# Sliding-window attention in pairs of steps: the same matmuls, grouped in sixteen rounds instead of thirty-two steps

## The chip, the cores and the metric

One core of a Trainium2 chip runs the kernel. A core has five engines with queues of their own: TensorE (PE) multiplies matrices, VectorE (DVE), ScalarE (ACT) and GpSimd (POOL) work elementwise, and SyncE (SP) issues most of the transfers. The metric is the time of one execution on the device, in microseconds (us); the median of three runs is given.

## What is computed

A trunk of two layers over 1024 tokens of width 1024, all in float32. Layer one is a gated linear recurrence, layer two is attention in a window of 128 keys; a gated feed-forward part with a short convolution follows each. The change lies in the attention of layer two, sixteen query heads of 64 that share four key and value heads:

```
def swa_sink_mixer(h, k, v, w_q, sinks, bias, mask, w_out):
    q = (h @ w_q).reshape(B, nb, SW_WINDOW, SW_KV_HEADS, SW_GROUP, SW_HEAD_DIM)
    ...
    kk, vv = with_prev(k), with_prev(v)
    logits = jnp.einsum('bntgrd,bnsgd->bngrts', q, kk).astype(jnp.float32) * scale
    ...
    logits = jnp.where(mask[None, :, None, None], logits, -jnp.inf)
    m = jnp.maximum(logits.max(-1), sink)
    p = jnp.exp(logits - m[..., None])
    denom = p.sum(-1) + jnp.exp(sink - m)
    o = jnp.einsum('bngrts,bnsgd->bntgrd', p, vv.astype(jnp.float32))
    o = o / jnp.moveaxis(denom, -1, 2)[..., None]
    return o.reshape(B, S, D).astype(h.dtype) @ w_out
```

Each query sees itself and the 127 tokens before it. `with_prev` puts the keys of the block before ahead of a block's own. So of the 256 keys that a block of 128 queries is multiplied with, exactly 128 count per query, the upper triangle of one block and the lower triangle of the other.

## The kernel before

**Precision.** A float32 product is made from three fast matmuls (`mm3`, lines 188 to 192): both operands are split into a high part and a low rest, and high by high, high by low and low by high are added. So every operand of a projection is first cast (ACT) and its low rest subtracted (DVE, `low_part`, line 162, which the profile shows as L164). The casts of weights from their raw tiles are line 171, other casts line 216. `T` holds the layer's input so, `HL` the weights.

**The attention, before.** The heads are taken in eight pairs, `c` = 0 to 7, and each pair in four steps `bp` of two blocks of 128 queries. `attend` (line 1299) is a generator that records one step in seven stages, with a `yield` after each:

1. Queries by keys on PE (line 1310, eight matmuls into one `psax` tile), and a copy of the diagonal block's logits to `X` on ACT (line 1313).
2. DVE copies the earlier block's logits into `X` under a triangular mask (line 1317), so that `X` holds each query's 128 valid logits; in a pair's first step, which has no earlier block, POOL masks (line 1320) instead. POOL adds the bias (line 1323).
3. DVE takes the maximum `nm` (lines 1328, 1331); `se`, the sink's part, is made on POOL for `c` up to 5, else on DVE (line 1332); ACT takes four exponentials of 128 by 128, each with its sum (line 1335), and the sink's (line 1337).
4. DVE makes the sum, its reciprocal and the product (lines 1339 to 1341).
5. PE transposes `X` in four (line 199).
6. DVE takes the two triangles apart into `W` (line 1349, two of 128 by 512); `W` is `W0` or row 7 of `Y`.
7. PE multiplies by the values (line 195, shown as sixteen records), and ACT copies the result to `Y` (line 1362), or, for the last pair, splits it into `T`.

**The fill.** Beside a step PE works on the next pair's queries: `q_proj` (line 1275) is a generator too, a half of the tokens takes eight `mm3` of 512 columns, and a quarter of a pair's 48 matmuls stands beside each step. `q_split` (line 1291) scales the finished half on ACT (line 1294, two) and takes its low part on DVE (line 1296, two). For the last pair the fill is the beginning of the output projection (`last_filler`, line 1376, which calls `out_part`). `q_unit` (line 1267) loads and splits a pair's query weights two pairs ahead; `out_unit` does so for the output weights.

**The order.** The order of PE, ACT, DVE and POOL in this part is the program's own, written out by hand: the loop over `c` and `bp` (line 1427) has up to three steps in flight beside the new one. In a step it records stages 1 and 2 of the new step, 7 of the step three back, 3 of the last one (ahead of the new one's stage 2), 5 and 6 of the step two back, a quarter of the fill, 4 of the last one, then splits of queries and a low part of a weight. `moves` (line 1425) says before which steps a part of `Y` is split into `T` for the output projection. What is left of the last three steps is written out behind the loop (line 1460 on), between parts of the output projection. Then `ffn` begins with `out_proj` (line 334), which adds the last head pair's part, and reads the residual rows that SP loads to `Y`.

**Buffers.** `X` has four buffers, `q` three, `psax` two of two PSUM banks and `psmm` four of one bank. A `psmm` bank serves in turn a half of the query projection, the transposes and the values.

Of the kernel before, what the change touches and what calls it, by code (L numbers as in the profile page):

```python
# [10 lines left out]
F32 = mybir.dt.float32  # L11
F32R = mybir.dt.float32r
U8 = mybir.dt.uint8
AF = mybir.ActivationFunctionType
# [93 lines left out]
def trunk(ctx: ExitStack, tc: tile.TileContext, a: dict, out: bass.AP):  # L108
# [1096 lines left out]
    with (tc.tile_pool(name="ta", bufs=1, reuse_waits="tile") as raws,  # L1205
# [90 lines left out]
                nc.vector.scalar_tensor_tensor(q[os, e, :], ps[es], 0.125, q[es, e, :].bitcast(F32),  # L1296
                                               op0=ALU.mult, op1=ALU.subtract)

        def attend(c, bp, q):
            pp, r = divmod(c, 4)  # L1300
            ps = psax()
            pv = ps.rearrange("p (e j s) -> p e j s", e=2, j=2)
            for low in range(2):
                for jj in range(2):
                    j = 2 * bp + jj
                    lo = P if j == 0 else 0
                    qs, ks = slice((j % 4) * P, (j % 4 + 1) * P), slice((j - 1) * P + lo, (j + 1) * P)
                    for e in range(2):
                        es = slice(64 * e, 64 * e + 64) if low else slice(0, P)
                        nc.tensor.matmul(pv[:, e, jj, lo:], q[bp // 2][es, e, qs],  # L1310
                                         Kl[es, pp, ks] if low else Kh[:, pp, e, ks], start=not low and jj == 0, stop=bool(low) and jj == 1)
            X = at.tile([P, 2, 2, P], F32, name="X", bufs=4)
            nc.scalar.copy(X, pv[:, :, :, P:])
            yield
            j0 = 1 if bp == 0 else 0
            for e in range(2):
                nc.vector.copy_predicated(X[:, e, j0:, :], msk[:, 7 * BL:].unsqueeze(1).to_broadcast([P, 2 - j0, P]),
                                          pv[:, e, j0:, :P])
                if j0:
                    nc.gpsimd.affine_select(out=X[:, e, 0, :], in_=X[:, e, 0, :], compare_op=ALU.is_ge,  # L1320
                                            fill=NEG, base=0, pattern=[[-1, P]], channel_multiplier=1)
            bv = bfs[c]
            nc.gpsimd.tensor_tensor(X, X, bv.unsqueeze(2).to_broadcast([P, 2, 2, P]), op=ALU.add)
            yield
            nm = sm.tile([P, 2, 2], F32, name="nm")
            se = sm.tile([P, 2, 2], F32, name="se")
            dn = sm.tile([P, 2, 2], F32, name="dn")
            nc.vector.tensor_reduce(nm, X, axis=mybir.AxisListType.X, op=ALU.max)
            skv = sk[:, 8 * pp + r:8 * pp + r + 5:4].unsqueeze(2).to_broadcast([P, 2, 2])
            nsv = nsk[:, 8 * pp + r:8 * pp + r + 5:4].unsqueeze(2).to_broadcast([P, 2, 2])  # L1330
            nc.vector.scalar_tensor_tensor(nm, nm, -1.0, nsv, op0=ALU.mult, op1=ALU.min)
            (nc.vector if c > 5 else nc.gpsimd).tensor_tensor(se, skv, nm, op=ALU.add)
            for e in range(2):
                for jj in range(2):
                    nc.scalar.activation(X[:, e, jj, :], X[:, e, jj, :], AF.Exp, bias=nm[:, e, jj:jj + 1],
                                         accum_out=dn[:, e, jj:jj + 1])
            nc.scalar.activation(se, se, AF.Exp)
            yield
            nc.vector.tensor_tensor(dn, dn, se, op=ALU.add)
            nc.vector.reciprocal(dn, dn)  # L1340
            nc.vector.tensor_tensor(X, X, dn.unsqueeze(3).to_broadcast([P, 2, 2, P]), op=ALU.mult)
            yield
            pt = psmm()
            for i in range(4):
                tr(pt[:, i * P:(i + 1) * P], X[:, i // 2, i % 2, :])
            yield
            W = W0 if bp % 2 else Y[:, NB - 1, :].rearrange("p (k g s) -> p k g s", k=2, g=4)
            for k in range(2):
                nc.vector.tensor_tensor(W[:, k], pt.rearrange("p (g s) -> p g s", g=4),
                                        tri[:, k, :].unsqueeze(1).to_broadcast([P, 4, P]), op=ALU.mult)  # L1350
            yield
            po = psmm()
            for jj in range(2):
                j = 2 * bp + jj
                for e in range(2):
                    kvc = (2 * pp + e) * 64
                    o = po[64 * e:64 * e + 64, jj * P:(jj + 1) * P]
                    mm32(o, Vt[:, j, kvc:kvc + 64], W[:, 0, 2 * e + jj, :], stop=j == 0)
                    if j:
                        mm32(o, Vt[:, j - 1, kvc:kvc + 64], W[:, 1, 2 * e + jj, :], start=False)  # L1360
            if c < 7:
                nc.scalar.copy(Y[:, c, bp * 256:(bp + 1) * 256], po[:, :256])
            else:
                ts = slice(bp * 256, (bp + 1) * 256)
                split(T[:, 0, c, ts], T[:, 1, c, ts], po[:, :256], lows)
            yield

        wo2 = a["swa_w_out"][0]
# [32 lines left out]
        with tc.manual_schedule(engines={EN.PE, EN.Activation, EN.DVE, EN.Pool}):  # L1401
            od.finish(lns[:4])
            late = [od.spawn(ln_rows(range(1), rows, 2.5, h2d), 6.0)]
            k_part(0)
            for tp in range(3):
                od.finish(lns[2 * tp:2 * tp + 2])
                if tp == 2:
                    late.append(od.spawn(ln_rows(range(1, NB), rows, 2.0, h2d)))
                v_part(tp)
            od.finish(lns[6:])  # L1410
            hl = q_unit(0)
            make_lows()
# [12 lines left out]
            moves = {26: (0, 2, 0, 4), 27: (2, 4, 0, 4), 28: (4, 6, 0, 4), 30: (6, 7, 0, 4)}  # L1425
            stage = lambda g: g and next(g)
            for c in range(8):
                fill = q_proj(hl) if c < 7 else last_filler()
                nq, nd = next(fill)
                for bp in range(4):  # L1430
                    it = attend(c, bp, q)
                    prev = [None] * (3 - len(flight)) + flight
                    if 4 * c + bp in moves:
                        Y_to_T(*moves[4 * c + bp], lows)
                    stage(it)
                    stage(prev[0])
                    stage(prev[2])
                    stage(it)
                    stage(prev[1])
                    stage(prev[1])  # L1440
                    stage(fill)
                    stage(prev[2])
                    while done:
                        q_split(*done.pop(0))
                    make_lows()
                    if bp == 0 and c < 6:
                        hl = q_unit(c + 2)
                    stage(fill)
                    if len(flight) > 2:
                        flight.pop(0)  # L1450
                    done.extend(nd)
                    nd.clear()
                    if c == 0 and bp == 1:
                        v_part(3)
                    if 0 <= 4 * c + bp - 21 < 4:
                        ring["hl"] = 4 * c + bp - 21
                        us.extend(out_unit(rows2, 4 * c + bp - 21, lows))
                    flight.append(it)
                q = nq
            a29, a30, a31 = flight  # L1460
            for _ in range(2):
                ps = psax()
                begun.extend([ps[:, :512], ps[:, 512:]])
            next(a31)
            next(a29)
            next(a30)
            next(a30)
            make_lows()
            Y_to_T(0, 4, 4, 8, lows)
            out_part(begun[2], us, 2, range(6))  # L1470
            next(a31)
            make_lows()
            next(a30)
            out_part(begun[2], us, 2, [6])
            next(a31)
            next(a31)
            make_lows()
            Y_to_T(4, 7, 4, 8)
            out_part(begun[3], us, 3, range(4))
            next(a31)  # L1480
            make_lows()
            out_part(begun[3], us, 3, range(4, 7))
            for tb in range(4, 6):
                out_part(begun[tb], us, tb, range(7))

# [32 lines left out]
```

## Time and profile before

| what | before |
|---|---|
| time, median of 3 runs (lowest to highest) | 2203.21 us (2203.15 to 2203.9) |
| time of the profiled execution | 2203.46 us |
| its span, first to last instruction | 2201.7 us |
| attention loop, first queries by keys to the last | 1289.8 to 1460.2 us |
| start of the output projection's last part | 1487.6 us |
| mean granted clock of TensorE | 0.996 |

The page of the profile gives each engine's busy time. More is told by the timeline, which lists an engine's instructions in order of time (start, length, engine, line of the kernel, operation, tile written from tile read, shape, count), with the idle time before one and what ended it in brackets. Neighbours of one kind are merged, with their count. An operation's length can overlap the next one's start on the same engine, so that the distance from start to start is what an engine spends on it. A busy PE is not PE at its peak: the ends of matmuls are modelled.

### The profile page before, as it was taken

The page shows a single profiled execution, that of the slowest core. Times are in us where ns is not written, and L with a number is a line of the kernel's source. Part 1 is how long each engine was busy: PE and PEld are TensorE (multiplying, and loading weights), DVE is VectorE, ACT ScalarE, POOL GpSimd, SP SyncE. Part 2 cuts the span into 40 slices and gives each one's busy share as a digit, 9 for nine tenths or more (in the row PEclk, how much of TensorE's full clock was granted, in tenths as well). Part 3 has the DMA queues.
Part 4 walks back from the last instruction along what each step waited for, and adds up shares of the span by engine and source line. Part 5 has one row for each costly group of instructions (what it writes and reads, how often), then busy time and mean ns, then how long its engine had stood idle before and what let it go on. Part 6 is the DMA issues. An engine that isn't in the chain of part 4 may idle for free.

```text
span 2201.7 us, 33408 instructions
## 1 busy us (share of the span) xinstructions
PE 2168.1 (98%) x13168; PEld 1811.4 (82%) x13168; DVE 1785.0 (81%) x2456; ACT 935.0 (42%) x1600; POOL 126.3 (6%) x161
## 2 busy tenths in 40 slices
PE   9999999989999999999999999999999999999998
PEld 8888888978788888887888888878888888887887
DVE  3777666565789888888998779977899888889987
ACT  3233333342744433444343456645544444343431
POOL 0000000030100000000000013211000000000001
PEclk9999999999999999999999999999999999999999
DMA  5654543244222222227854431123133222249663
GB/s 195 230 173 154 192 135 110 79 71 141 86 77 88 86 87 86 86 88 257 290 174 142 106 99 35 35 86 121 62 98 104 86 72 74 86 153 309 207 221 129
DMA packets 231972, 281.15 MB, mean 128 GB/s; under 512 B 30008, under 2 KB 160776, under 8 KB 229000
## 3 DMA queue, kind: packets, MB, share of 16 engines
q1 hardware_dynamic: 228736, 276.53, 38.8%
q10 hardware_dynamic: 2888, 2.45, 0.9%
q8 instruction: 103, 1.69, 0.3%
q14 instruction: 53, 0.43, 0.1%
q0 software_dynamic: 192, 0.04, 0.0%
HBM read 213.96 MB, written 65.01 MB: 127 GB/s over the span
## 4 chain that ended last, share of the span: by engine, by line
PE 80%; DVE 10%; ACT 3%; DMA 3%; issue 2%; POOL 1%; SPq 0%; DVEq 0%; ACTq 0%; POOLq 0%
PE psmm L189 16%; PE psmm L191 16%; PE psmm L190 16%; PE psax L191 8%; PE psax L189 8%; PE psax L190 8%; PE psax L195 3%; DVE T L164 1%; DVE HL L164 1%; PE psax L199 1%; PE psmm L195 1%; PE psax L1310 1%; DMA raw<-in_hgrn_w_out_dram 1%; ACT Y L264 1%; DMA rx<-in_ffn_w_in_dram 1%
## 5 line engine op out<-in xcount | busy, mean ns | idle before, releaser
L189 PE MATMUL psmm<-T,HL 128*128 128x512 f32 x768 | 307.2, 400 | 0.0
L190 PE MATMUL psmm<-T,HL 128*128 128x512 f32 x768 | 300.1, 391 | 2.0 <-DVE T L164 2.0
L191 PE MATMUL psmm<-T,HL 128*128 128x512 f32 x768 | 300.7, 392 | 0.0
L494 DVE SCALAR_TENSOR_TENSOR Y<-Y,cwt 128x1023 f32<-128x1023 f32 (+1 forms) x176 | 225.1, 1279 | 40.1 <-ACT Y L492 39.8
L492 ACT ACTIVATE Y<-Y,cwt 128x1024 f32<-128x1024 f32 x88 | 109.0, 1238 | 263.6 <-DVE Y L481 259.5
L189 PE MATMUL psmm<-HL,T 128*128 128x256 f32 (+1 forms) x656 | 200.1, 305 | 0.0
L191 PE MATMUL psmm<-HL,T 128*128 128x256 f32 (+1 forms) x656 | 195.7, 298 | 1.1 <-DVE T L164 1.1
L190 PE MATMUL psmm<-HL,T 128*128 128x256 f32 (+1 forms) x656 | 195.6, 298 | 0.0
L216 ACT CAST HL<-rx 128x1024 fp32r<-128x1024 f32 (+1 forms) x137 | 140.3, 1043 | 121.8 <-DMA rx<-in_ffn_w_in_dram 35.2
L164 DVE TENSOR_TENSOR HL<-rx,HL 128x1024 fp32r<-128x1024 f32 (+1 forms) x137 | 165.6, 1211 | 13.9 <-ACT HL L216 13.7
L190 PEld LDWEIGHTS psmm<-T,HL 128*128 128x128 f32 x768 | 144.4, 188 | 31.1 <-DVE T L164 2.9
L191 PEld LDWEIGHTS psmm<-T,HL 128*128 128x128 f32 x768 | 144.1, 188 | 31.1
L189 PEld LDWEIGHTS psmm<-T,HL 128*128 128x128 f32 x768 | 144.3, 188 | 30.2 <-issue 0.4
L191 PE MATMUL psax<-T,HL 128*128 128x512 f32 x352 | 137.6, 391 | 0.0
L189 PE MATMUL psax<-T,HL 128*128 128x512 f32 x352 | 137.5, 391 | 0.0
L190 PE MATMUL psax<-T,HL 128*128 128x512 f32 x352 | 137.4, 390 | 0.0
L189 PEld LDWEIGHTS psmm<-HL,T 128*128 128x128 f32 x656 | 126.9, 193 | 6.2 <-issue 2.5
L191 PEld LDWEIGHTS psmm<-HL,T 128*128 128x128 f32 x656 | 126.7, 193 | 4.7 <-DVE T L164 1.5
L190 PEld LDWEIGHTS psmm<-HL,T 128*128 128x128 f32 x656 | 127.0, 194 | 3.2
L164 DVE TENSOR_TENSOR HL<-raw,HL 128x1024 fp32r<-128x1024 f32 x52 | 63.8, 1228 | 81.0 <-ACT HL L171 80.7
L238 POOL TENSOR_TENSOR rs<-rs,nhalf 128x1 f32<-128x1 f32 x32 | 26.0, 813 | 1292.3 <-DVE rs L237 1291.8
L216 ACT CAST HT<-rx 128x1024 fp32r<-128x1024 f32 (+1 forms) x51 | 43.9, 860 | 88.5 <-PE psmm L190 30.4
(303 smaller groups left out, 5224.5 us busy)
## 6 DMA issues: line engine op xcount, KB each, us to landing
rx<-in_ffn_w_in_dram SPq DMA_DIRECT2D x136, 256.0 KB, 3.5
rx<-gd SPq DMA_DIRECT2D x118, 256.0 KB, 3.5
Y<-in_ffn_w_out_dram SPq DMA_DIRECT2D x44, 512.0 KB, 6.1
bsd<-Y SPq DMA_DIRECT2D x22, 1024.0 KB, 4.3
gd<-Y SPq DMA_DIRECT2D x44, 512.0 KB, 2.7
rx<-in_ffn_w_out_dram SPq DMA_DIRECT2D x54, 256.0 KB, 4.0
R<-bsd SPq DMA_DIRECT2D x44, 256.0 KB, 3.7
Y<-in_ffn_w_in_dram SPq DMA_DIRECT2D x40, 256.0 KB, 3.2
```

What stands on the lines that cost most here:

```text
L164: make = lambda e: e.tensor_tensor(lo, src, hi.bitcast(F32), op=ALU.subtract)
L189: nc.tensor.matmul(ps, st(0), mv(0), start=start, stop=False)
L190: nc.tensor.matmul(ps, st(0), mv(1), start=False, stop=False)
L191: nc.tensor.matmul(ps, st(1), mv(0), start=False, stop=stop)
L195: nc.tensor.matmul(ps, lhsT, rhs, start=start, stop=stop, **kw)
L199: nc.tensor.transpose(ps, src, ident)
L216: nc.scalar.copy(hi, src)
L238: nc.gpsimd.tensor_tensor(rs, rs, nhalf, op=ALU.pow)
L264: nc.scalar.activation(hf[:, kc, :], ps[:, k * P:(k + 1) * P], AF.Identity, bias=shift, scale=scale)
L492: nc.scalar.activation(c, u, AF.Identity, bias=cwt[:, l, 3, ci:ci + 1], scale=cwt[:, l, 2, ci:ci + 1])
L494: nc.vector.scalar_tensor_tensor(c[:, sh:], u[:, :S - sh], cwt[:, l, 2 - sh, ci:ci + 1], c[:, sh:], op0=ALU.mult, op1=ALU.add)
L1310: nc.tensor.matmul(pv[:, e, jj, lo:], q[bp // 2][es, e, qs], Kl[es, pp, ks] if low else Kh[:, pp, e, ks], start=not low and jj == 0, stop= ...
```

## The change

A generator now records a pair of steps, `m` = 0 to 15: `c` is `m // 2`, and `half` says whether it is the first or the second half of the tokens. `attend(m, q)` has six stages, each for both steps: queries by keys and copies; masks and bias; maxima and exponentials; sums and products; transposes and `W` (stages 5 and 6 of before in one); values and their copy, 128 by 512 instead of two of 128 by 256. `se` is always made on DVE. In a round, the loop records stages 1 and 2 of the new pair, the transposes and `W` of the pair before, stages 3 and 4 of the new one, weight casts, a whole half of the fill (24 matmuls), `q_split` of this half at once, the low parts, and the values of the pair before. So one pair is in flight beside the new one. The moves from `Y` to `T` are two, of four and of three pairs, and stand between stages 3 and 4 of rounds 13 and 14; the weight units stay at the same pairs. The tail is written anew. Tiles and buffers are the same, and so is the number of matmuls.

The core of it, in the changed kernel's lines:

```
-        def attend(c, bp, q):
+        def attend(m, q):
+            c, half = divmod(m, 2)
             pp, r = divmod(c, 4)
+            steps = (2 * half, 2 * half + 1)
+            pvs, Xs = [], []
+            for bp in steps:
+                ps = psax()
...
+                            nc.tensor.matmul(pv[:, e, jj, lo:], q[half][es, e, qs],
...
+                X = at.tile([P, 2, 2, P], F32, name="X", bufs=4)
+                nc.scalar.copy(X, pv[:, :, :, P:])
+            yield
+            for bp, pv, X in zip(steps, pvs, Xs):
...
+                    nc.vector.copy_predicated(X[:, e, j0:, :], ...)
...
+                nc.gpsimd.tensor_tensor(X, X, bv.unsqueeze(2).to_broadcast([P, 2, 2, P]), op=ALU.add)
+            yield
+            for X in Xs:
...
+                nc.vector.tensor_reduce(nm, X, axis=mybir.AxisListType.X, op=ALU.max)
+                nc.vector.scalar_tensor_tensor(nm, nm, -1.0, nsv, op0=ALU.mult, op1=ALU.min)
-            (nc.vector if c > 5 else nc.gpsimd).tensor_tensor(se, skv, nm, op=ALU.add)
+                nc.vector.tensor_tensor(se, skv, nm, op=ALU.add)
...
+                        nc.scalar.activation(X[:, e, jj, :], X[:, e, jj, :], AF.Exp, bias=nm[:, e, jj:jj + 1], ...)
+                nc.scalar.activation(se, se, AF.Exp)
+            yield
+            for X, (dn, se) in zip(Xs, dens):
+                nc.vector.tensor_tensor(dn, dn, se, op=ALU.add)
+                nc.vector.reciprocal(dn, dn)
+                nc.vector.tensor_tensor(X, X, dn.unsqueeze(3).to_broadcast([P, 2, 2, P]), op=ALU.mult)
+            yield
+            for X in Xs:
+                pts.append(psmm())
+                for i in range(4):
+                    tr(pts[-1][:, i * P:(i + 1) * P], X[:, i // 2, i % 2, :])
+            Ws = [Y[:, NB - 1, :].rearrange("p (k g s) -> p k g s", k=2, g=4), W0]
+            for pt, W in zip(pts, Ws):
+                for k in range(2):
+                    nc.vector.tensor_tensor(W[:, k], ...)
+            yield
+            po = psmm()
...
+            if c < 7:
+                nc.scalar.copy(Y[:, c, ts], po)
+            else:
+                split(T[:, 0, c, ts], T[:, 1, c, ts], po, lows)
             yield
...
-            moves = {26: (0, 2, 0, 4), 27: (2, 4, 0, 4), 28: (4, 6, 0, 4), 30: (6, 7, 0, 4)}
+            moves = {13: [(0, 4, 0, 4)], 14: [(4, 7, 0, 4)]}
+            prev = None
+            for m in range(16):
+                c, half = divmod(m, 2)
+                if half == 0:
+                    fill = q_proj(hl) if c < 7 else last_filler()
+                    nq, nd = next(fill)
+                it = attend(m, q)
+                next(it)
+                next(it)
+                if prev:
+                    next(prev)
+                next(it)
+                for args in moves.get(m, []):
+                    Y_to_T(*args, lows)
+                make_lows()
+                next(it)
+                if half == 0 and c < 6:
+                    hl = q_unit(c + 2)
+                if 10 <= m < 14:
+                    ring["hl"] = m - 10
+                    us.extend(out_unit(rows2, m - 10, lows))
+                for _ in range(4):
+                    next(fill)
+                while nd:
+                    q_split(*nd.pop(0))
+                make_lows()
+                if m == 0:
+                    v_part(3)
+                if prev:
+                    next(prev)
+                if half:
+                    q = nq
+                prev = it
...
+            Y_to_T(0, 4, 4, 8, lows)
+            make_lows()
+            out_part(begun[2], us, 2, range(7))
+            next(prev)
+            Y_to_T(4, 7, 4, 8)
+            make_lows()
+            out_part(begun[3], us, 3, range(7))
+            next(prev)
+            make_lows()
             for tb in range(4, 6):
                 out_part(begun[tb], us, tb, range(7))
```

More of the change, by code (lines that the diff above doesn't have):

```diff
@@ L1312, in attend @@
[L1312 to L1330, printed above, removed]
@@ L1340, in attend @@
[L1340 to L1360, printed above, removed]
+                        kvc = (2 * pp + e) * 64
@@ L1424, in trunk @@
             us = []
-            moves = {26: (0, 2, 0, 4), 27: (2, 4, 0, 4), 28: (4, 6, 0, 4), 30: (6, 7, 0, 4)}
[L1426 to L1459, printed above, removed]
```

77 lines of the change are left out of this document (41 added, 36 removed).

## The prediction

> **What bounds the kernel now.** I read the page first: its span, the busy shares.
>
> ```profile
> span 2201.7 us, 33408 instructions
> PE 2168.1 (98%) x13168; PEld 1811.4 (82%) x13168; DVE 1785.0 (81%) x2456; ACT 935.0 (42%) x1600; POOL 126.3 (6%) x161
> ```
>
> TensorE (PE) is never free for long, so the whole kernel goes at PE's pace. The profiled execution took 2203.46 us, 1.76 more than its span; the median of the three timed runs is 2203.21, 0.25 lower, which I neglect. But a share of the whole says nothing about one stage, so next I cut out the attention with the busy times by stretch. One head pair (four steps) is 1354.80 to 1375.89; the last two rows are the end of the loop.
>
> ```profile
> 1354.80:1375.89 21.09, 21.09 (x157) 17.30 (x156) 19.09 (x42) 13.74 (x49) 6.56 (x10) 1.00 0.12 32
> 1418.00:1439.00 21.00, 20.37 (x153) 16.37 (x152) 20.05 (x42) 15.31 (x47) 5.46 (x7) 1.00 0.07 20
> 1439.00:1460.00 21.00, 18.85 (x133) 14.95 (x133) 20.24 (x46) 12.29 (x46) 6.77 (x6) 1.00 0.00 1
> ```
>
> The columns are length, then busy time and instructions of PE, weight load, VectorE (DVE), ScalarE (ACT) and GpSimd (POOL), then clock. PE is busy for all of 21.09 us, and DVE already for 19.09. At the end DVE has 20.05 and 20.24 of 21, and PE begins to lose time (0.63 and 2.15 us). So DVE is close behind PE: it keeps up only as long as it almost never waits.
>
> The timeline of PE gives one step of 5.35 us: 12 projection matmuls ("fill") 2.86, queries by keys 1.01, values 1.07, transposes 0.41 (each to the next start).
>
> ```profile
> 1357.26 0.48 PE L189 MATMUL psmm<-T,HL 128*128 128x512 f32 x1
> ...
> 1359.89 0.40 PE L191 MATMUL psmm<-T,HL 128*128 128x512 f32 x1
> 1360.12 0.64 PE L1310 MATMUL psax<-Kh,q 128*128 128x256 f32 x4
> 1360.69 0.51 PE L1310 MATMUL psax<-Kl,q 64*128 64x256 f32 x4
> 1361.13 1.14 PE L195 MATMUL psmm<-Y,Vt 128*64 128x128 f32 x16
> 1362.20 0.66 PE L199 MATMUL psmm<-ident,X 128*128 128x128 f32 x4
> 1362.61 0.48 PE L189 MATMUL psmm<-T,HL 128*128 128x512 f32 x1
> ```
>
> **The change part by part.** *PE.* The matmuls are the same in number and size; a round now has two steps' queries by keys, both transposes of the round before, 24 fill matmuls, both steps' values. A switch between groups costs about 0.1: within the fill the starts lie 0.23 apart (1359.89 to 1360.12), which makes 2.76 for twelve, and it takes 2.86. Of eight switches per pair four go: a gain between nothing and 0.4 us per round. I take 0.3, so PE needs 10.3 us per round, against 10.6 for two steps now (half of 21.09).
>
> *DVE and ACT.* Here the order changes. Now the exponentials of a step run while DVE masks the next step and multiplies W of the one before; three steps are in flight. Afterwards everything of a pair stands in one line. DVE's order in a round: masks (four), W of the pair before (four), maxima of A and B, sums and products of A and B, the two low halves of q (line 1296), the low half of a weight unit. ACT's order: eight exponentials, weight cast, two scales of q, copy of values, two copies of X. Both queues are in order, so the round closes in a loop: the first mask of the next round stands behind the q lows, these behind the q scales on ACT, these behind all eight exponentials, these behind the maxima, these behind W and the masks. Durations, start to start, from the timelines of DVE and of ACT:
>
> ```profile
> 1381.23 1.41 DVE L1296 SCALAR_TENSOR_TENSOR q<-psmm,q 64x512 fp32r<-64x512 f32 x2
> 1382.67 0.69 DVE L1328 TENSOR_REDUCE nm<-X 128x4 f32<-128x512 f32 x1
> 1383.39 0.17 DVE L1331 SCALAR_TENSOR_TENSOR nm<-nm,nsk 128x4 f32<-128x4 f32 x1
> 1383.59 0.78 DVE L1317 COPY_PREDICATED X<-msk,psax 128x256 f32<-128x256 uint8 x2
> 1384.26 1.27 DVE L1349 TENSOR_TENSOR W<-psmm,tri 128x512 f32<-128x512 f32 x2
> 1385.46 0.39 DVE L1339 TENSOR_TENSOR dn<-dn,se 128x4 f32<-128x4 f32 x1
> 1385.88 0.18 DVE L1340 RECIPROCAL dn<-dn 128x4 f32<-128x4 f32 x1
> 1386.09 0.69 DVE L1341 TENSOR_TENSOR X<-X,dn 128x512 f32<-128x512 f32 x1
> 1386.70 1.22 DVE L164 TENSOR_TENSOR HL<-raw,HL 128x1024 fp32r<-128x1024 f32 x1
> 1387.84 0.68 DVE L1328 TENSOR_REDUCE nm<-X 128x4 f32<-128x512 f32 x1
> ```
>
> ```profile
> 1379.97 1.19 ACT L1294 ACTIVATE q<-psmm 64x512 fp32r<-64x512 f32 x2
> 1381.18 1.05 ACT L171 CAST HL<-raw 128x1024 fp32r<-128x1024 f32 x1
> 1382.33 0.59 ACT L1313 COPY X<-psax 128x512 f32<-128x512 f32 x1
> 1383.68 0.40 ACT L1335 ACTIVATE X<-X,nm 128x128 f32<-128x128 f32 x1
> ...
> 1385.24 0.19 ACT L1337 ACTIVATE se<-se 128x4 f32<-128x4 f32 x1
> ```
>
> Masks 2 x 0.67 = 1.34; W 2 x 1.20 = 2.40; maximum 0.72 + 0.20 = 0.92; hand-over to ACT 0.1; eight exponentials and two sums 2 x 1.56 + 0.2 = 3.3; q scales 1.20; hand-over 0.07; q lows 1.44. **An odd round's loop is 10.8 us.** An even round also has the weight unit, cast 1.0 on ACT and low 1.14 on DVE, both in the same line, and its first step masks half as much (0.49 instead of 0.78, row below): **12.6 us**. A head pair takes 23.4 instead of 21.09, because PE's 2 x 10.3 no longer sets it.
>
> What is hidden: the maximum of B with its three small ones (0.72 + 3 x 0.2, of which the se that moves from POOL to DVE is 0.2) under A's exponentials, 1.56; the additions on POOL (1.30, row below, two per round) under W, 2.40; the products (dn 0.2 like nm, 0.21, 0.61: 1.02 each) under the second exponentials and the q scales; copy of values and of X (about 0.5 + 0.59) under the q lows. Should a cover go, each costs its own length, at most 0.5 us a round. PE meets the loop twice a round: its transposes wait for the products, its first fill matmul for the copy of values on ACT (its PSUM bank was that of the values one round ago). The weight and bias loads on SP's queue keep their places and land rounds ahead.
>
> ```profile
> 1298.69 0.69 DVE L1328 TENSOR_REDUCE nm<-X 128x4 f32<-128x512 f32 x1 [1.47 <-POOL X L1323]
> L1323 POOL TENSOR_TENSOR X<-X,bf x32: 1269/1300/1314, 1297.4 to 1462.2; 128x512 f32<-128x512 f32 x32
> 1421.72 0.49 DVE L1317 COPY_PREDICATED X<-msk,psax 128x128 f32<-128x128 uint8 x2
> 1467.57 1.91 ACT L216 CAST T<-Y 128x2048 fp32r<-128x2048 f32 x1
> 1469.51 2.29 DVE L164 TENSOR_TENSOR T<-Y,T 128x2048 fp32r<-128x2048 f32 x1 [0.38 <-ACT T L216]
> 1471.03 1.48 ACT L216 CAST T<-Y 128x1536 fp32r<-128x1536 f32 x1
> 1473.64 1.75 DVE L164 TENSOR_TENSOR T<-Y,T 128x1536 fp32r<-128x1536 f32 x1
> 1487.57 0.39 PE L189 MATMUL psmm<-HL,T 128*128 128x512 f32 x1
> ```
>
> *The sum.* Round 0: maximum at 1298.7, +0.92, exponentials 3.3, cast 1.0, q scales 1.2, q lows 1.44, low 1.14: masks of round 1 start at 1307.8. Rounds 1 to 9: 5 x 10.8 + 4 x 12.6 = 104.4. Rounds 10 to 12 also split an output weight (1.0 + 1.14): 14.7 + 12.9 + 12.6 (12 has no query weight) = 40.2. Round 13 puts four heads' move to T between exponentials and products: 8.1 to the end of the exponentials, cast 1.91, low 2.21, products 2 x 1.02, q lows 1.44, low 1.14 = 16.8. Round 14: 7.8 + cast 1.48 + low 1.75, for which PE waits in mid-fill; then 10 fill matmuls 2.3, values 1.9, queries by keys 1.1, copy 0.6: 16.9. So the masks of round 15 start at 1486.1, its queries by keys 1.7 earlier, 1484.4. From there PE runs through: 102 matmuls x 0.229 = 23.4, queries by keys 1.9, transposes 1.6, values 3.9, switches 0.3: 31.1. The output projection's last part starts at 1515.5; now it is 1487.57 (last row). **+27.9 us.**
>
> *The clock* is a term that the loop doesn't hold. In rounds 13 and 14 PE stands idle for about 16.8 - 10.3 = 6.5 us. What such a gap does stands elsewhere in this trace:
>
> ```profile
> 477.61 0.97 PE L195 MATMUL psax<-qp,kp 128*32 128x32 f32 x54 [4.75 <-issue]
> 478.51 0.58 PE L189 MATMUL psmm<-HL,T 128*128 128x256 f32 x1
> 480.00:482.00 2.00, 2.00 (x11) 2.00 (x11) 2.00 (x3) 0.07 (x1) 1.85 (x1) 0.50 0.27 38
> 482.30 0.36 PE L191 MATMUL psmm<-HL,T 128*128 128x256 f32 x1
> ```
>
> After 4.75 us idle the clock is 0.50. Eighteen matmuls of 256 columns start from 478.51 to 482.30, 3.79 us for 17 intervals; at half of a 512-column one's 0.23 they would take 1.96, and a switch 0.1: 1.7 us lost. The slow stretch of round 13 ends in the next wait; that of round 14 delays round 15. I take 1.7, between 0 and 3.4. Sum: 27.9 + 1.7 = 29.6, hence **2203.46 + 29.6 = 2233 us**. The Trainium skill, "TensorE: Matmul & The Clock Gate", Part 1, says that the clock halves after an idle window of about 3.4 us and comes back after as long a busy one. The trace agrees in kind (4.75 us idle, some 4 us slow); by this rule the waits of up to 1.3 us in rounds 1 to 12 cost no clock, and an estimate from the page for one gap (3.4 us at half speed) would again be 1.7.
>
> **The rivals.** *Faster: PE still sets the pace.* Only the switches count, 16 x 0.3 = 4.8 us, with 0.4 each 6.4: 2197 to 2198.7. It decides at an average loop of 10.3 us per round. For it: DVE's own work in an odd round is 9.5 us. Against: the loop holds 3.3 + 1.2 us of ACT in which DVE has only the two products, and nothing in the diff lets a q low pass.
> *Only the end pays:* the steady rounds overlap more than I think and hold 21.1 per head pair; five pairs x 2.3 = 11.5 us less, 2222. For it: PE's queue of rounds could absorb some; against: a loop drifts until it is the bound.
> *No difference:* gain of the switches and loss at the end cancel, 2203; the end alone (rounds 13 and 14, 33.7 against 2 x 10.6) loses 12 us, so hardly.
> *Later still:* the residual rows and late output weights on SP's queue start behind the last values, and the projection waits for them.
>
> ```profile
> 1477.31 16.65 SPq L159 DMA_DIRECT2D rx<-in_swa_w_out_dram  x16
> ```
>
> Sixteen loads in 16.65 us are 4.2 us for a unit of four; one or two units late make 2237 to 2241. Against: the queue starts on them 10.3 us ahead of the projection now (1477.31, 1487.57), and the last values, at which it could start, end about 10 us ahead of it in the sum above (42 matmuls x 0.229).
>
> **How the numbers follow.** My forecast 0.80, later still 0.06, only the end 0.07, no difference 0.03, faster 0.04. All durations 5% off move the loss by about 5 us, the clock by 1.7 either way, and half a microsecond a round of lost cover would be 7: 2224 to 2242; this takes in a part of "later still". 0.2% is 4.4 us, about what a measurement can tell from no change: faster (below 2198.8) 0.04, same 0.03, slower 0.93.
>
> **What would show it.** The first queries by keys of two head pairs lie 23.4 apart instead of 21.09; PE's idle time between 1290 and 1516 grows from about 3 us to 35 to 40, released by the products (line 1355) ahead of transposes and by ACT (line 1380) ahead of fill; two gaps of 6 us or more in the last rounds, with the clock at 0.50 behind them. In the first rounds ACT's queue must show exponentials, scales of q and copies without a gap, while DVE waits ahead of its q lows. If the head pairs stay at 21, the loop is wrong; if they take 23.4 and the time is below 2222, my sum of the end is.

## The result, and the profile after

| | before | after |
|---|---|---|
| time, median (lowest to highest) | 2203.56 us (2203.15 to 2204.04, 4 runs) | 2233.99 us (2232.46 to 2236.31, 4 runs) |
| ratio after to before, 95% interval | | 1.0144 [1.0132, 1.0156] |
| profiled execution | 2203.46 us | 2234.04 us |

The changed kernel is slower by 1.4%; 2233.0 us was forecast, with 2224 to 2242 as the range. The first two lines of the page of after:

```profile
span 2232.2 us, 33370 instructions
PE 2177.4 (98%) x13168; PEld 1815.1 (81%) x13168; DVE 1785.0 (80%) x2476; ACT 929.1 (42%) x1582; POOL 120.4 (5%) x137
```

All busy times are about as they were, and PE still has 98%. The page as a whole hides what happened, so the same view as before is the next step: busy times by stretch, one head pair (two rounds) of after. Columns are length, then busy time and instructions of PE, PEld, DVE, ACT, POOL, then clock, DMA share, GB/s.

```profile
1359.71:1382.89 23.18, 21.67 (x159) 17.20 (x157) 19.11 (x45) 12.95 (x48) 5.65 (x6) 1.00 0.08 23
```

Before, a head pair took 21.09 us, with PE busy for all of it. Now it takes 23.18, DVE is busy for the same 19.1, and PE is free in between. Where PE waits is told by its groups of instructions between 1290 and 1516 us (line, operation, tiles; busy, mean ns; idle time ahead of the group and what ended it):

```profile
L189 PE MATMUL psmm<-T,HL 128*128 128x512 f32 x112 | 46.0, 411 | 4.0 <-ACT Y L1380 4.0
L199 PE MATMUL psmm<-ident,X 128*128 128x128 f32 x128 | 19.5, 288 | 12.8 <-DVE X L1355 11.7 <-ACT X L1347 0.6
L189 PE MATMUL psmm<-HL,T 128*128 128x256 f32 (+1 forms) x30 | 11.7, 390 | 7.3 <-ACT T L216 7.3
```

There are two places in every head pair, the transposes waiting for the products and the fill waiting for ACT's copy, and two large waits at the end: 5.68 of the 12.8 us are one wait for products in round 13, and the 7.3 are one for `T` in round 14. These are the places that the prediction names. The loop itself is seen on DVE (timeline of after, from the first mask of an odd round to that of the next odd one):

```profile
1354.32 1.44 DVE L1327 COPY_PREDICATED X<-msk,psax 128x256 f32<-128x256 uint8 x4
...
1363.56 1.39 DVE L1296 SCALAR_TENSOR_TENSOR q<-psmm,q 64x512 fp32r<-64x512 f32 x2
1364.96 1.18 DVE L1327 COPY_PREDICATED X<-msk,psax 128x128 f32<-128x128 uint8 x4
...
1373.23 0.69 DVE L1355 TENSOR_TENSOR X<-X,dn 128x512 f32<-128x512 f32 x1
1374.86 1.39 DVE L1296 SCALAR_TENSOR_TENSOR q<-psmm,q 64x512 fp32r<-64x512 f32 x2 [0.93 <-PE psmm L199]
1376.28 1.23 DVE L164 TENSOR_TENSOR HL<-raw,HL 128x1024 fp32r<-128x1024 f32 x1
1377.54 1.44 DVE L1327 COPY_PREDICATED X<-msk,psax 128x256 f32<-128x256 uint8 x4
...
1448.85 1.39 DVE L1296 SCALAR_TENSOR_TENSOR q<-psmm,q 64x512 fp32r<-64x512 f32 x2 [0.93 <-ACT q L1294]
```

and on ACT in the even round that starts at 1364.96:

```profile
1369.41 0.40 ACT L1347 ACTIVATE X<-X,nm 128x128 f32<-128x128 f32 x1 [4.34 <-DVE nm L1343]
...
1372.69 1.03 ACT L171 CAST HL<-raw 128x1024 fp32r<-128x1024 f32 x1
1373.63 1.19 ACT L1294 ACTIVATE q<-psmm 64x512 fp32r<-64x512 f32 x2
1374.85 0.59 ACT L1380 COPY Y<-psmm 128x512 f32<-128x512 f32 x1
```

ACT waits 4.34 us for the maxima, then does exponentials, weight cast, scales of `q` and the copy back to back. In this round DVE in turn waits with its low parts until 1374.86, when the scales end (1373.63 + 1.19). The row names PE as the releaser; but the low parts read what the scales have written, and for the same wait of 0.93 us in round 12 (1448.85) the view names these scales. Behind the low parts stand the next masks. The odd round (1354.32 to 1364.96) takes 10.64 us, the even one 12.58.

The odd round closes by two ways at once. Its low parts (1363.56) show no wait: they stand directly behind DVE's second product, which ends at 1363.52, and ACT's scales of that round end at 1363.48. The products, which the prediction had as hidden, are there as long as the scales.

The masks' starts over the whole loop, for the sum (rounds 1, 10, 13, 14, 15):

```profile
1307.89 0.77 DVE L1327 COPY_PREDICATED X<-msk,psax 128x256 f32<-128x256 uint8 x2
...
1411.39 0.84 DVE L1327 COPY_PREDICATED X<-msk,psax 128x128 f32<-128x128 uint8 x3
...
1451.49 0.77 DVE L1327 COPY_PREDICATED X<-msk,psax 128x256 f32<-128x256 uint8 x2
...
1468.48 0.85 DVE L1327 COPY_PREDICATED X<-msk,psax 128x128 f32<-128x128 uint8 x3
...
1488.47 0.78 DVE L1327 COPY_PREDICATED X<-msk,psax 128x256 f32<-128x256 uint8 x2 [7.00 <-ACT X L1319]
```

and PE in the last rounds, with the two long waits, the queries by keys of round 15 and the output projection's last part:

```profile
1464.83 2.21 PE L199 MATMUL psmm<-ident,X 128*128 128x128 f32 x8 [5.68 <-DVE X L1355]
...
1477.71 0.79 PE L189 MATMUL psmm<-HL,T 128*128 128x512 f32 x1 [7.26 <-ACT T L216]
...
1479.50 0.79 PE L191 MATMUL psmm<-HL,T 128*128 128x512 f32 x1 [0.57 <-DVE T L164]
...
1486.64 0.74 PE L1315 MATMUL psax<-Kh,q 128*128 128x256 f32 x4
...
1517.99 0.39 PE L189 MATMUL psmm<-HL,T 128*128 128x512 f32 x1
```

The last row was at 1487.57 before: 30.4 us later, and the profiled time is 30.6 longer. So almost the whole loss lies ahead of this point.

### The profile page after: what moved, and what is told of

Read it like the earlier page. It is cut to its first block, busy times and chain, and to the rows that moved or that the text cites. A ratio compares the mean times of both kernels' runs of the same rounds, so it can differ in the third digit from the quotient of the medians.

```text
span 2232.2 us, 33370 instructions
## 1 busy us (share of the span) xinstructions
PE 2177.4 (98%) x13168; PEld 1815.1 (81%) x13168; DVE 1785.0 (80%) x2476; ACT 929.1 (42%) x1582; POOL 120.4 (5%) x137
## 4 chain that ended last, share of the span: by engine, by line
PE 78%; DVE 11%; ACT 5%; issue 3%; DMA 2%; POOL 1%; SPq 0%; DVEq 0%; ACTq 0%; POOLq 0%
PE psmm L189 16%; PE psmm L191 16%; PE psmm L190 16%; PE psax L191 8%; PE psax L190 8%; PE psax L189 8%; PE psax L195 3%; ACT X L1347 1%; PE psax L199 1%; DVE HL L164 1%; DMA raw<-in_hgrn_w_out_dram 1%; ACT Y L264 1%; DVE T L164 1%; ACT T L216 1%; DVE X L1327 1%
## 5 line engine op out<-in xcount | busy, mean ns | idle before, releaser
L1347 ACT ACTIVATE X<-X,nm 128x128 f32<-128x128 f32 x128 | 49.6, 388 | 85.2 <-DVE nm L1343 85.2
```

## The experiments

The theory: a round is closed by one chain that alternates between DVE and ACT (masks, W, maxima, exponentials, scales of `q`, low parts of `q`, next masks), longer than PE's work of a round; the last rounds add the moves to `T` to it, and long waits there halve PE's clock. The rivals: PE is slower in rounds of two steps as such; or the loss is only in the last rounds; or the extra work on DVE (`se`) counts.

| kernel | median, us | ratio to before, 95% interval | head pair, us |
|---|---|---|---|
| after | 2233.99 | 1.0144 [1.0132, 1.0156] | 23.2 |
| low parts and scales of `q` put off | 2211.65 | 1.0046 [1.003, 1.0061] | 21.1 |
| only the low parts put off | 2216.53 | 1.006 [1.0043, 1.0077] | 21.4 |
| two copies behind the exponentials | 2243.77 | 1.019 [1.0175, 1.0205] | 24.6 |
| two copies ahead of them | 2233.94 | 1.014 [1.0123, 1.0157] | 23.2 |
| moves ahead of the exponentials | 2223.72 | 1.0101 [1.0087, 1.0115] | 23.2 |
| output projection reordered | 2224.63 | 1.0105 [1.009, 1.012] | 23.2 |
| scales, low parts and moves | 2208.4 | 1.003 [1.0019, 1.0042] | 21.1 |
| these three and the reordering | 2200.57 | 0.9994 [0.9985, 1.0003] | 21.1 |
| before, `se` on DVE | 2202.59 | 1.0005 [0.9996, 1.0014] | 21.1 |
| thirty idle matmuls in round 14 | 2231.05 | 1.0129 [1.0113, 1.0144] | 23.2 |
| eighteen | 2234.99 | 1.0146 [1.0131, 1.0161] | 23.2 |

A head pair is the distance between its first queries by keys and the next pair's, in the steady rounds. The kernels were measured in four groups, in which before itself had medians of 2203.56 (with after), 2202.13, 2201.95 and 2202.70 us; each ratio is to before of its own group. A difference of medians between groups is therefore good to some 1.6 us only.

### Cutting the loop

`q_split` is divided into `q_high` (ACT) and `q_low` (DVE); a finished half is held until the next round.

```diff
                 it = attend(m, q)
                 next(it)
+                for half_q in held:
+                    q_high(*half_q)
                 next(it)
                 if prev:
                     next(prev)
                 next(it)
...
+                while held:
+                    q_low(*held.pop(0))
                 make_lows()
...
-                while nd:
-                    q_split(*nd.pop(0))
+                held.extend(nd)
+                nd.clear()
```

> The changed kernel, with the scaling of a finished half of the queries taken out of the round that makes it: its two scales on ACT stand ahead of the next round's exponentials, its two low parts on DVE between the next round's maxima and products. Nothing else moves. Theory (the round is closed by DVE's low parts behind ACT's scales behind the exponentials): the loop is cut, PE sets the pace, head pairs lie 20.6 us apart instead of 23.2, eight of them give back about 21 us and the shift of the end somewhat more: about 2209, between 2205 and 2213; what is left is the wait at the moves of rounds 13 and 14. Rival A (PE itself is slower in rounds of two steps, for instance by its tiles in PSUM): head pairs stay at 23, 2232 to 2236. Rival B (the loss is only at the end): the same, 2232 to 2236.

Measured 2211.65 us, inside the range. A head pair of this kernel, busy times by stretch:

```profile
1353.60:1374.69 21.09, 21.09 (x158) 17.16 (x157) 19.10 (x46) 13.34 (x47) 5.71 (x6) 1.00 0.11 32
```

PE is busy without a gap again, with the same instructions on every engine as after; only a round's two scales and two low parts stand at another place. So rounds of two steps cost PE nothing by themselves, and 22.3 us of the loss by the medians (21.6 by the ratios), some seven tenths, go with the loop; both rivals, which expected no change, fall. What is left is the end: waits of 3.66 us for the products and 5.24 us for `T`:

```profile
1443.85 2.09 PE L199 MATMUL psmm<-ident,X 128*128 128x128 f32 x8 [3.66 <-DVE dn L1360]
1455.09 0.80 PE L189 MATMUL psmm<-HL,T 128*128 128x512 f32 x1 [5.24 <-ACT T L216]
```

But the expected 20.6 per head pair is missed: it is 21.09, what it was before. On that more below.

The same with only the low parts put off, to the same place; ACT's scales stay in their own round:

```diff
-                while nd:
-                    q_split(*nd.pop(0))
+                for half_q in nd:
+                    q_high(*half_q)
+                held.extend(nd)
+                nd.clear()
```

> The changed kernel, with only DVE's two low parts of the queries put off into the next round (between its maxima and products); ACT's two scales stay behind the exponentials of their own round. Theory (the chain is closed where DVE's low parts wait for ACT's scales ahead of the next masks): one cut is enough, head pairs lie 21.1 us apart as with both put off, and the time is the same, about 2211, between 2208 and 2214. Rival (what matters is that ACT's scales stand behind the exponentials and hold the next round's work on ACT up): the head pairs stay near 23 and the time above 2225.

Measured 2216.53, outside the range, though far nearer to the theory's side: 17.5 of the 22.3 us come back. One cut does open the loop, but the next one behind it is then late at once. DVE's row at a round's masks in this kernel:

```profile
1380.15 1.27 DVE L1334 COPY_PREDICATED X<-msk,psax 128x128 f32<-128x128 uint8 x4 [0.92 <-ACT X L1326]
```

The masks now wait for ACT's copies of `X`, which stand behind the scales and the copy of the values in ACT's order. Those copies were hidden under the low parts, as the prediction had it; once the low parts are gone the cover is gone too. A head pair takes about 21.4 us, and the rounds that split output weights lose more.

### Lengthening the loop

Two copies of 128 by 256 on ACT, from a constant to an unused tile, added in every round, in one kernel at the first of these places and in another at the second:

```diff
                 if prev:
                     next(prev)
+                for _ in range(2):
+                    nc.scalar.copy(idle, tri.rearrange("p a b -> p (a b)"))
                 next(it)
+                for _ in range(2):
+                    nc.scalar.copy(idle, tri.rearrange("p a b -> p (a b)"))
                 for args in moves.get(m, []):
```

> The changed kernel, with work added that changes nothing of the output: two copies of 128 by 256 on ACT in every round, recorded behind the eight exponentials, so inside the loop of exponentials, scales of q and low parts. A copy of 128 by 512 takes 0.59 us from start to start, two of half the width are about 0.6 to 0.7. Theory (this chain is what closes the round): every one of 16 rounds becomes longer by all of it, 2244, between 2241 and 2247, though ACT is busy for only 42 per cent of the time. Rival (PE, or the total of DVE's work, sets the round): 2234, as ACT has the room.

> The same two copies on ACT in every round, but recorded ahead of the exponentials, where ACT waits for DVE's maxima. Theory: they run in that wait and cost nothing, 2233 to 2236. Rival (ACT's total work counts, not its place in the line): the same as with the copies behind the exponentials.

Measured 2243.77 us behind, 2233.94 ahead. One head pair of each, behind first:

```profile
1337.32:1361.75 24.43, 21.81 (x158) 17.19 (x157) 18.97 (x44) 14.21 (x51) 5.68 (x6) 1.00 0.13 28
```

```profile
1358.73:1381.91 23.18, 21.68 (x159) 17.20 (x157) 19.12 (x46) 14.39 (x52) 5.69 (x6) 1.00 0.10 24
```

ACT has the same 14.2 to 14.4 us of work in both, and DVE and PE have theirs of after; only behind the exponentials does it cost. There, on ACT's timeline, the two copies take 0.73 us (1364.34 to 1365.07). In the other kernel they stand in ACT's wait for the maxima, which is 3.58 us instead of 4.34 and ends as it did:

```profile
1364.34 0.82 ACT L1457 COPY idle<-tri 128x256 f32<-128x256 f32 x2
1365.07 1.19 ACT L1295 ACTIVATE q<-psmm 64x512 fp32r<-64x512 f32 x2
```

```profile
1368.44 0.40 ACT L1348 ACTIVATE X<-X,nm 128x128 f32<-128x128 f32 x1 [3.58 <-DVE nm L1344]
```

Twice 0.73 is 1.46 per head pair; this one grew by 1.2, the next two by 1.4. In 16 rounds ACT, which is busy for 42% of the time, gets 11.7 us more to do; 9.8 of them go into the total, because of where they stand.

### The end

The moves from `Y` to `T` recorded ahead of a round's maxima and exponentials:

```diff
                 if prev:
                     next(prev)
-                next(it)
                 for args in moves.get(m, []):
                     Y_to_T(*args, lows)
+                next(it)
                 make_lows()
                 next(it)
```

> The changed kernel, with the moves from Y to T of rounds 13 and 14 recorded ahead of the round's maxima and exponentials instead of behind them, so that ACT's cast to T runs while DVE does the masks and W. Theory: only rounds 13 and 14 are mended, by about the length of the two casts on the line (1.9 and 1.5 us) and the slow clock behind one of them (2 us): about 2228, between 2226 and 2231; head pairs stay at 23.2. Rival (the end is the loss): more than half of the 30 us comes back, below 2218. Rival (PE is slower as such): no difference, 2234.

Measured 2223.72: 10.3 us come back instead of 6, outside the range, though the reason holds and head pairs stay at 23.2. DVE's low parts of `T` in after, then the masks of round 14 and the low parts in this kernel:

```profile
1461.38 2.29 DVE L164 TENSOR_TENSOR T<-Y,T 128x2048 fp32r<-128x2048 f32 x1 [4.11 <-ACT T L216]
1477.69 1.76 DVE L164 TENSOR_TENSOR T<-Y,T 128x1536 fp32r<-128x1536 f32 x1 [3.70 <-ACT T L216]
```

```profile
1454.82 2.28 DVE L164 TENSOR_TENSOR T<-Y,T 128x2048 fp32r<-128x2048 f32 x1
...
1462.02 1.18 DVE L1327 COPY_PREDICATED X<-msk,psax 128x128 f32<-128x128 uint8 x4
...
1467.45 1.75 DVE L164 TENSOR_TENSOR T<-Y,T 128x1536 fp32r<-128x1536 f32 x1
```

From the masks of round 14 to its low part of `T` it is 9.2 us in after (1468.48, 1477.69) and 5.4 here. My sum took only the casts off the line; with the casts done early, DVE also no longer waits out the exponentials before it does the low parts (4.11 and 3.70 us of waiting), so that these 2.3 and 1.8 us lie beside the exponentials instead of behind them. PE's long waits fall from 5.68 and 7.26 us to 1.10 and 4.30.

The beginning of the output projection in another order, so that what needs only the first move comes first for both halves:

```diff
-            out_part(begun[0], us, 0, range(2))
...
-            out_part(begun[1], us, 1, [6])
-            yield
+            for tb, kcs in ((0, range(2)), (0, range(2, 4)), (1, range(2)), (1, range(2, 4)),
+                            (0, range(4, 6)), (1, range(4, 6)), (0, [6]), (1, [6])):
+                out_part(begun[tb], us, tb, kcs)
+                yield
```

> The changed kernel, with only the beginning of the output projection reordered, so that parts which need the second move come later. Theory: PE's wait in round 14 goes (it has 3.7 us more of other matmuls in front of it), the head pairs stay at 23.2 apart: about 2230, between 2227 and 2232. Rival (the wait only moves to the next place): 2234.

Measured 2224.63: 9.4 us come back, again more than the 4 that I expected, and outside the range. The wait of 7.26 us for `T` is gone, and with it the slow clock behind it, which I had left out of the expectation; what is left are 4.92 and 2.42 us, for the products of rounds 13 and 14, so that PE's waits there add up to 7.3 us instead of 13.5. Behind the 2.42 the clock is again 0.51, from 1478.70 to 1482.00.

The two cuts of the loop together with the early moves, and this with the reordering:

> Both edits together: the scaling of the queries deferred into the next round, and the moves recorded ahead of the exponentials. Theory: the loop and most of the wait at the end are gone, about 2205, between 2202 and 2209, within half a per cent of the kernel before. Rival (rounds of two steps cost PE or PSUM something that no order mends): 2215 or more.

> Both edits, and the beginning of the output projection in another order: first those parts of both halves of the tokens that need only the head pairs moved in round 13, then those that need the three moved in round 14. Theory: PE then has 16 more fill matmuls (3.7 us) to do in front of the second move, the last wait goes, and what stays is the gain of the fewer switches on PE, 16 times about 0.3: about 2198.5, between 2196 and 2202, so faster than the kernel before by about 0.2 per cent. Rival (DVE's work of the last rounds sets the end in any order): no better than both edits alone, 2203 to 2209.

Measured 2208.4 and 2200.57 us, both inside their ranges. The gains don't add up: the early moves are worth 10.3 us in the changed kernel, but 3.3 once the loop is cut. In the kernel without reordering PE still waits 5.93 us for the low part of the second move, and in the last one no wait in the loop is longer than 0.93 us. This version is as fast as the kernel before, 0.9994 [0.9985, 1.0003]; that it would be faster, as I expected, isn't shown. With the losses of the new order mended, its fewer switches on PE bring nothing that can be measured: the 4.8 us that were taken for them (16 times 0.3) would be 0.9978, outside the interval, while up to 3.3 us are not excluded.

### The parts that were costed at nothing or nearly so

`se` on DVE in all steps, in the kernel before:

```diff
-            (nc.vector if c > 5 else nc.gpsimd).tensor_tensor(se, skv, nm, op=ALU.add)
+            nc.vector.tensor_tensor(se, skv, nm, op=ALU.add)
```

> The kernel before, with one part of the change alone: the sum for the sink (se) is made on DVE in all steps instead of on POOL in the first 24. Theory: DVE has 0.2 us more per step and PE's idle time hides it, 2203 to 2205. Rival (this work on the busiest engine beside PE is a part of the loss): 24 times 0.2, 2208.

Measured 2202.59, ratio 1.0005 [0.9996, 1.0014]: no difference. The rival's 1.0022 is outside the interval. This shows it for the order of before; no run takes `se` off DVE in the changed kernel.

The clock: matmuls whose results are overwritten, ahead of the product that waits for the second move (30, or 18):

```diff
             out_part(begun[0], us, 0, range(2, 4))
             yield
+            for _ in range(30):
+                nc.tensor.matmul(begun[1], T[:, 0, 0, :P], us[0][:, 0, :], start=True, stop=True)
             out_part(begun[0], us, 0, range(4, 6))
```

> The changed kernel, with thirty matmuls of 512 columns more on TensorE in round 14, in front of the product that waits for the second move; their results are overwritten and change nothing of the output. They fill the 7.26 us wait almost (30 times 0.229 is 6.9 us). Theory (behind the wait the clock is 0.50 and about 11 matmuls go at half pace): the clock stays at 1.00, the first queries by keys of round 15 come about 2.3 us earlier after the wait's end, 2231.7. Rival (the slow start behind the wait is set by DVE's and ACT's parts of T, not by the clock): no difference, 2234, or 30 matmuls too many: 2236.

> The same with eighteen matmuls (4.1 us), which leave some 3 us of the wait idle. Theory: the clock falls for a shorter stretch or not at all, 2232 to 2233. Rival: no difference, 2234.

Measured 2231.05 and 2234.99. The intervals of the first and of after overlap, so the times alone don't settle it; the traces do. From the matmul that the low part of `T` releases to the queries by keys of round 15 it is 7.14 us in after (1479.50, 1486.64). With thirty matmuls, and the mean clock of the stretch from the end of the cast on:

```profile
1476.37 0.50 PE L191 MATMUL psmm<-HL,T 128*128 128x512 f32 x1 [0.56 <-DVE T L164]
...
1480.84 0.39 PE L1315 MATMUL psax<-Kh,q 128*128 128x256 f32 x1
```

```profile
1475.19:1480.84 5.65, 5.09 (x46) 3.77 (x44) 3.01 (x7) 0.00 (x0) 0.00 (x0) 1.00 0.01 3
```

4.47 us at full clock: **the slow clock cost 2.7 us**, not the 1.7 that I had put down. With eighteen matmuls nothing is gained, which I had not expected: after 3.06 and 1.06 us of idle time PE is as slow as in after, and the same stretch takes 7.25 us (1478.05 to 1485.30). At 1476.25, behind the first of the two waits, it is not slow yet:

```profile
1476.25 0.50 PE L189 MATMUL psmm<-HL,T 128*128 128x512 f32 x1 [3.06 <-ACT T L216]
...
1478.05 0.79 PE L191 MATMUL psmm<-HL,T 128*128 128x512 f32 x1 [1.06 <-DVE T L164]
...
1485.30 0.73 PE L1315 MATMUL psax<-Kh,q 128*128 128x256 f32 x4
```

## Why the prediction was right, point by point

- **DVE and ACT close the round: shown.** Forecast 10.8 and 12.6 us per odd and even round, 23.4 per head pair; measured 10.64 and 12.58, 23.2. Putting the low parts and scales elsewhere gives 21.09, adding 0.73 us a round into the chain lengthens a steady head pair by 1.4 of 1.46 us (mean of four), adding it beside the chain does nothing. Counting a round by walking along the chain, instead of comparing busy times, was the step that decided.
- **What is hidden: right, but with nothing to spare.** `se` costs nothing in the order of before; in after it lies beside ACT's exponentials, for which DVE then waits 0.7 us. The copies of `X` lie under the low parts, as the kernel without these showed by losing the cover. In odd rounds the products end 0.04 us behind the scales, so there they are a second way by which the round closes; no run separates the two. The 0.9 us that was missing over rounds 1 to 9 comes from the odd rounds, 0.16 shorter than the sum of its parts.
- **The sum: right in nearly every term,** from masks to masks. Round 1 at 1307.8, measured 1307.89; rounds 1 to 9 104.4, measured 103.5; 10 to 12 40.2, measured 40.1; 13 16.8, measured 17.0; 14 16.9 plus 1.7 of clock, measured 20.0, the one term that is off by more than a microsecond (1.0 of the 1.4 us is clock); from the queries by keys of round 15 to the last part 31.1, measured 31.35. The start of the last part was put at 1515.5 + 1.7 = 1517.2 and is 1517.99. That it is so close is in part luck: the loop came out 0.9 us shorter and round 14 1.4 us longer.
- **The clock: right in kind, the term too small.** 1.7 was taken from a gap of 4.75 us elsewhere; the runs give 2.7 for round 14. The slow stretch behind round 13's wait cost nothing, as the prediction had it: PE is back at full pace at 1468.45, and the next wait takes the delay up. That the short waits of rounds 1 to 12 cost no clock is wrong as a rule: in round 12 of after the clock fell too (shown at the end), though the sum shows no loss by it, as PE doesn't set the pace there.
- **The gain of the switches: wrong.** I took 0.3 us a round from PE's work, and 10.3 for a round. Without the loop it is 21.09 for two rounds, what the four steps took before. It did no harm to the forecast, since PE didn't set the pace, but the rival "faster" (2197 to 2198.7) had no ground: at its best the new order gives 2200.57, no difference. PE's timeline of the kernel with the loop cut shows where the gain went:

```profile
1375.77 0.74 PE L1322 MATMUL psax<-Kh,q 128*128 128x256 f32 x4
1376.44 0.50 PE L1322 MATMUL psax<-Kl,q 64*128 64x256 f32 x4
1376.87 1.09 PE L199 MATMUL psmm<-ident,X 128*128 128x128 f32 x8
1377.72 0.47 PE L189 MATMUL psmm<-T,HL 128*128 128x512 f32 x1
...
1383.38 1.15 PE L195 MATMUL psmm<-Y,Vt 128*64 128x128 f32 x16
1384.31 1.09 PE L195 MATMUL psmm<-W,Vt 128*64 128x128 f32 x16
1385.33 0.74 PE L1322 MATMUL psax<-Kh,q 128*128 128x256 f32 x4
```

  The fill of a round takes 5.66 us to the next start (1377.72 to 1383.38; twice 2.86 before), the values 1.95 (twice 1.07): 0.25 gained. The transposes take 0.85 (twice 0.41), and a step's queries by keys 1.10 instead of 1.01, of which the first four take 0.67 instead of 0.57: 0.2 lost. Why these are slower, when they follow others of their kind or the values instead of the fill, no run here tells.
- **"PE's idle time grows to 35 to 40 us": wrong.** The three groups shown above hold 24.1 us. The profile counts a matmul as busy to its modelled end, and counts slow ones in full: for one head pair PE is shown busy for 21.67 us in after, for the same matmuls that take 21.09, without a gap, with the loop cut. Shown idle time understates a loss; the distance between like instructions doesn't.
- **Two gaps at the end:** 5.68 and 7.26 us, the first a little under the 6 or more that were forecast for both, with the clock at 0.50 behind both.
- **No difference and only the end pays: false.** The loop's share is 22.3 us when it is cut alone; mending the end alone gives 10.3. These overlap by about 7 us (together 25.6): cutting the loop alone already shortens the two long waits by 4.0 us, from 5.68 and 7.26 to 3.66 and 5.24. Where the other 3 us lie isn't shown. **Later still:** the last part started 31.35 us behind the queries by keys of round 15, PE's own work there, and behind its start only 0.2 us of the loss is left (30.4 of 30.6), so SP's loads were not late.

## What to carry to other kernels

When steps are merged into larger rounds on queues that run in order, write down each engine's queue for one round and walk along the waits from one instruction to the same one in the next round; if that chain is longer than the busiest engine's work, it is the time of the round, however idle the engines on it are. The cure is to put off one link into the next round, where its input has long been ready, and then to look at once for the link behind it. At such a point a change that saves nothing on the busiest engine can at best come back to where it started.

## What the runs showed of the hardware

The clock fell to 0.50 after far less idle time than I had thought safe. In the kernel with early moves two waits were enough, and the clock stayed low for the fill behind them:

```profile
1458.26 0.63 PE L199 MATMUL psmm<-ident,X 128*128 128x128 f32 x4 [1.10 <-DVE dn L1353]
1459.28 0.63 PE L199 MATMUL psmm<-ident,X 128*128 128x128 f32 x4 [0.39 <-ACT q L1294]
```

```profile
1460.50:1463.50 3.00, 3.00 (x8) 2.32 (x8) 2.97 (x7) 1.68 (x2) 1.27 (x3) 0.50 0.01 3
```

In after, waits of 1.00 or 1.01 us ahead of the transposes, one in each head pair up to round 11, left it at 1.00 (the head pair shown above has 1.00 throughout), and so did one of 1.37 us ahead of the fill of round 11. In round 12 another of 1.01 stands between waits of 0.58 and 0.79 us, and behind the three the clock fell for about 3.4 us:

```profile
1437.60:1440.40 2.80, 2.80 (x8) 2.20 (x7) 2.79 (x6) 0.15 (x1) 1.07 (x3) 0.50 0.00 0
```

In the kernel with copies behind the exponentials the head pair shown above has 1.00 too, the next one 0.93, though its waits are no longer:

```profile
1361.75:1386.36 24.61, 23.29 (x159) 18.24 (x157) 19.11 (x46) 14.39 (x52) 5.66 (x6) 0.93 0.09 22
```

The Trainium skill, "TensorE: Matmul & The Clock Gate", Part 1, speaks of an idle window of about 3.4 us, free-running, ahead of a drop; these runs show drops behind waits that are each shorter, 1.10 and 0.39 us in one kernel, 3.06 and 1.06 in another, 0.58, 1.01 and 0.79 in after, so that a wait's length alone doesn't tell whether it costs clock. What else decides (where the wait falls in such a window would be one reading) was not tried.
